# The seven products' sums on GpSimd, in another order, and a third seven-product chunk in five feed-forward layers

## The chip, the cores and the metric

The kernel runs on one core of a Trainium2 chip. The core has engines that run side by side, each with its own queue of instructions, worked off in order: TensorE (PE: matmuls; PEld: the load of the stationary operand), VectorE (DVE), ScalarE (ACT) and GpSimd (POOL), and SyncE (SP), which here issues the transfers from memory (DMA). They wait for each other by semaphores. SBUF is the on-chip memory, 128 partitions wide; PSUM is the small memory into which TensorE writes.

The metric is the device time of one execution in microseconds (us), as a median of runs.

## What is computed

One sequence of 256 tokens (two tiles t of 128 rows) with 1024 features goes through a first block and two layers of a second one, in float32:

```python
# first block
h = h + 0.5 * rms_norm(swiglu(rms_norm(h, g), w_gate, w_up, w_down), g2)   # f1
h = h + rms_norm(hybrid_mixer(rms_norm(h, g)), g2)    # attention and pooling, w_in 1024 x 4096
h = h + 0.5 * rms_norm(swiglu(...), g2)               # f2
h = h + rms_norm((p @ w_proj) * sigmoid(rms_norm(h, g) @ w_gate), g2)
# second block, i = 0, 1 (mixer: gated linear attention, then retention)
h = layer_norm(a * h + 0.5 * swiglu_2(h, ...))        # s0, s2
h = layer_norm(a * h + mixer(h))
h = layer_norm(a * h + 0.5 * swiglu_2(h, ...))        # s1, s3

def swiglu(x, w_gate, w_up, w_down):                  # 1024 -> 2816 -> 1024
    return (silu(x @ w_gate) * (x @ w_up)) @ w_down
```

So there are six feed-forward layers (f1, f2, s0 to s3). The other parts matter here only as neighbours.

## The kernel before

**Units and the three-matmul product.** The weights come in units of 128 x 2048 float32 (1 MB, four blocks of 128 rows by 512 columns). A unit is loaded into a `raw` buffer (five of them), ScalarE casts it to a rounded copy `whi` (float32r), VectorE subtracts that from `raw` and rounds the rest to `wlo` (`fetch`, lines 174 and 177; five buffers of each). The activations are split in the same way. `mm3` (lines 217 to 219) makes each product of three matmuls: hi by hi, hi by lo, lo by hi, 128x512 each.

**Chunks.** The gate and up products of a feed-forward layer have 5 chunks of 512 columns (0 to 4) and a last of 256 for each. A plain chunk takes four units (two halves of the 1024 rows, gate and up), and for both row tiles 4 x 2 x 4 x 3 = 96 matmuls.

**Seven products.** For the chunks in `SEVEN` (line 73; chunks 2 and 4 of f2 and s0 to s3) the two row tiles, the two halves of the inner dimension, and gate and up are taken as a 2 x 2 by 2 x 2 block product, made in the Strassen-Winograd way from seven products in place of eight (`seven`, lines 369 to 404): 7 x 4 x 3 = 84 matmuls. It needs sums of the four units a, b, c, d (`fetch_sum`, lines 182 to 198, table `SUMS`): in the order of the products a, a+b, b+c, a+b+c, c, d, a+b+c+d, where each of the four sums is a VectorE add in place (line 194), directly ahead of its cast (line 196) and subtraction (line 197). It also needs four differences of the activations (`sums_in`, lines 302 to 316), made and split on VectorE and ScalarE, once a layer. The products are combined on VectorE from PSUM (lines 392 to 402). Two pairs of column chunks of the mixer's input projection and two of the retention's go through the same functions (`Chunks.pair`, line 553), which makes 14 such groups in all.

**Order.** The program is written out in one order; each engine takes its own instructions in that order. `unit` (line 200) hands out the next unit and first issues the fetches up to four units ahead when a summed unit is near (line 204). `defer(n, f)` puts small work `n` ticks later (a tick is six matmuls), `settle` brings deferred work forward until a condition holds. In a seven-product chunk the finish (`finish7`, line 469) takes gate and up of one row tile together.

Of the kernel before, what the change touches and what calls it, by code (L numbers as in the profile page):

```python
# [11 lines left out]
F32 = mybir.dt.float32  # L12
# [3 lines left out]
AF = mybir.ActivationFunctionType  # L16
ALU = mybir.AluOpType
AX = mybir.AxisListType

P = 128  # L20
# [5 lines left out]
CW = 512  # L26
# [6 lines left out]
LAG = 3  # L33
POOL_WINDOWS = (2, 4, 8, 16)
EDGE = 8
SUMS = (("a", None), ("a", "b"), ("b", "c"), ("a", "c"), ("c", None), ("d", None), ("a", "d"))
AHEAD = 2
TURN = (5, 7)
SPIN = 9
# [12 lines left out]
def ffn_units(g, u, d, seven=()):  # L52


    out = []
    for c in range(5):
        four = [(g, 2 * c), (g, 2 * c + 1), (u, 2 * c), (u, 2 * c + 1)]
        out += [(four, j) for j in range(7)] if c in seven else four
    return out + [(g, 10), (g, 11)] + [(d, i) for i in range(11)]


def chunk_units(name, order):

    out = []
    for c in order:
        if isinstance(c, tuple):
            out += [([(name, 2 * b + i) for b in c for i in range(2)], j) for j in range(7)]
        else:
            out += [(name, 2 * c + i) for i in range(2)]
    return out  # L70


SEVEN = (2, 4)
MIX_ORDER = [1, 0, 2, 3, (4, 5), (6, 7)]
GLA_ORDER = [1, 0, 2, 4, 3, 5]
RET_ORDER = [2, 3, 0, 1, 4, 8, (5, 9), 6, 10, (7, 11)]
# [2 lines left out]
def all_units():  # L79

    p = ffn_units("f1g", "f1u", "f1d")
    p += chunk_units("bin", MIX_ORDER) + [("bpl", 0), ("bat", 0), ("bpl", 1), ("bat", 1)] + [("bout", i) for i in range(4)]
    p += ffn_units("f2g", "f2u", "f2d", SEVEN)
    p += [("pgate", i) for i in range(4)] + [("pproj", 0)]
    p += ffn_units("s0g", "s0u", "s0d", SEVEN)
    p += chunk_units("gin", GLA_ORDER) + [("gout", i) for i in range(4)]
    p += ffn_units("s1g", "s1u", "s1d", SEVEN) + ffn_units("s2g", "s2u", "s2d", SEVEN)
    p += chunk_units("rin", RET_ORDER) + [("rout", i) for i in range(8)]
    return p + ffn_units("s3g", "s3u", "s3d", SEVEN)


class Build:
# [89 lines left out]
    def fetch_sum(self, four, j):  # L182


        nc = self.nc
        if j == 0:
            self.sums = {}
        r = self.sums
        for key, at in {0: (("a", 0), ("b", 2)), 2: (("c", 3),), 5: (("d", 1),)}.get(j, ()):
            r[key] = self.T("raw", [P, UNIT], F32)  # L190
            nc.sync.dma_start(out=r[key], in_=self.ins[four[at][0]][four[at][1]])
        key, other = SUMS[j]
        if other:
            nc.vector.tensor_tensor(out=r[key], in0=r[key], in1=r[other], op=ALU.add)  # L194
        hi, lo = self.T("whi", [P, UNIT], F32R), self.T("wlo", [P, UNIT], F32R)
        nc.scalar.copy(hi, r[key])  # L196
        nc.vector.tensor_tensor(out=lo, in0=r[key], in1=hi.bitcast(F32), op=ALU.subtract)  # L197
        return Split(hi, lo)

    def unit(self, name, i, kb, ahead=1):  # L200
# [28 lines left out]
    def split(self, src, n=4, name="xT"):  # L229

        hi = self.S([P, n, P], F32R, name + "h")
        lo = self.S([P, n, P], F32R, name + "l")
        v = src[:, :n * P].rearrange("p (a b) -> p a b", a=n)
        self.nc.scalar.copy(hi, v)  # L234
        self.nc.vector.tensor_tensor(out=lo, in0=v, in1=hi.bitcast(F32), op=ALU.subtract)  # L235
        return Split(hi, lo)
# [62 lines left out]

        self.defer(TURN[t] + n + (more if raws is not None else 0), turn)  # L300

    def sums_in(self, raws, tag):

        a11, a12, a21, a22 = (raws.pop((t, n)) for t in range(NT) for n in range(2))
        y = {}
        for i, o, a, b in ((1, a22, a21, a22), (3, a21, a11, a21), (2, a11, a11, a22), (4, a12, a12, a11)):
            self.nc.vector.tensor_tensor(out=o, in0=a, in1=b, op=ALU.subtract)
            if i < 3:
                both = self.T(("gp", "gq")[i - 1], [P, 2, 4, P], F32R, name="yT")
                hi, lo = both[:, 0], both[:, 1]  # L310
            else:
                hi, lo = (self.T(tag, [P, CW], F32R, name=n).rearrange("p (a b) -> p a b", a=4) for n in ("yTh", "yTl"))
            self.nc.scalar.copy(hi, o)
            self.nc.vector.tensor_tensor(out=lo, in0=o, in1=hi.bitcast(F32), op=ALU.subtract)
            y[i] = Split(hi, lo)
        return y

    def rms_post(self, t, acc, gpost, half):

# [49 lines left out]
    def seven(self, x, y, four, done):  # L369

        nc, TT = self.nc, self.nc.vector.tensor_tensor
        t = lambda tag, name: self.T(tag, [P, CW], F32, name=name)

        def times(name, x, j):
            ps = self.M(name)
            w = self.unit(four, j, 4, 4)
            for k in range(4):
                self.mm3(ps, x[:, k, :], w[:, k, :], k == 0, k == 3)  # L380
                if k % 2:
                    self.tick()
            return ps

        p1, u2, u4, c22 = t("u", "p1"), t("u", "u2"), t("y", "u4"), t("y", "c22")
        nc.scalar.copy(p1, times("P1", x[0][0], 0))
        yield
        p5 = times("P5", y[1], 1)
        yield
        p7 = times("P7", y[3], 2)  # L390
        yield
        TT(out=u2, in0=times("P6", y[2], 3), in1=p1, op=ALU.subtract)
        TT(out=u4, in0=p5, in1=u2, op=ALU.add)
        TT(out=c22, in0=u4, in1=p7, op=ALU.subtract)
        TT(out=u2, in0=u2, in1=p7, op=ALU.subtract)
        yield
        TT(out=u4, in0=times("P3", y[4], 4), in1=u4, op=ALU.add)
        yield
        TT(out=p1, in0=times("P2", x[0][1], 5), in1=p1, op=ALU.add)
        done(0, p1, u4)  # L400
        yield
        TT(out=u2, in0=times("P4", x[1][1], 6), in1=u2, op=ALU.subtract)
        done(1, u2, c22)
        yield

    def lagged(self, x, name, n_units, after, lag=LAG, have=None, extra=None):
# [42 lines left out]
    def ffn(self, xT, r, wg, wu, wd, after, first=False, raws=None):  # L449
        nc = self.nc  # L450
# [16 lines left out]
                self.defer(4, lambda: hT.__setitem__((t, c), self.splitT(pr, n // P, "hT")))  # L467

        def finish7(c):
            prs = []  # L470

            def done(t, a, b):
                sg = self.T("sg", [P, CW], F32)
                pr = self.T("sg", [P, CW], F32, name="pr")
                nc.scalar.activation(sg, a, AF.Silu)
                nc.vector.tensor_tensor(out=pr, in0=b, in1=sg, op=ALU.mult)
                prs.append(pr)
                if t:
                    self.defer(4, lambda: turn(c, CW, *prs))

            return done

# [2 lines left out]
        def turn(c, n, *prs):  # L485
            tps = [self.transpose4(pr, n // P, "hT") for pr in prs]
            for t in range(NT):
                hT[t, c] = self.split(tps[t], n // P, "hT")

        pss, y = {}, {}  # L490
# [25 lines left out]
            finish(0, t, pss[t, wg], pss[t, wu], CW)  # L516
        for c in range(1, 6):
            if raws is not None and c == 1:
                self.defer(4, lambda: y.update(self.sums_in(raws, "ld")))
            if raws is not None and c in SEVEN:  # L520
                self.settle(lambda: y)
                for _ in self.seven(xT, y, [(wg, 2 * c), (wg, 2 * c + 1), (wu, 2 * c), (wu, 2 * c + 1)], finish7(c)):
                    pass
                continue
            for nm in (wg, wu) if c < 5 else (wg,):
                for i in range(2):
                    w = [self.unit(nm, 2 * c + i, 4, 3 if raws is not None else 2)]
                    for t in range(NT):
                        if i == 0:
                            pss[t, nm] = self.M()  # L530
                        self.proj(pss[t, nm], xT[t], w, CW, 4, 4 * i, KD)
                for t in range(NT):
                    if c == 5:
                        finish(c, t, pss[t, nm][:, :256], pss[t, nm][:, 256:], 256)
                    elif nm == wu:
                        finish(c, t, pss[t, wg], pss[t, wu], CW)
        self.lagged(lambda t, k: hT[t, k // 4][:, k % 4, :], wd, 11, after, have=lambda t, k: (t, k // 4) in hT)

    class Chunks:
# [8 lines left out]
            self.w, self.ps, self.over, self.y, self.groups = {}, {}, set(), {}, {}  # L548

        def sums(self):  # L550
            self.y.update(self.b.sums_in(self.raws, "S"))

        def pair(self, c):

            if c not in self.groups:
                self.b.settle(lambda: self.y)

                def done(t, *outs):
                    for i in range(2):
                        self.done(c[i], t, outs[i])  # L560
                        self.over.add((c[i], t))

                self.groups[c] = self.b.seven(self.xT, self.y, [(self.name, 2 * i + j) for i in c for j in range(2)], done)
            next(self.groups[c])
# [656 lines left out]
```

## Time and profile before

| | |
|---|---|
| median of three runs | 1611.38 us (1611.19 to 1611.48) |
| the profiled execution | 1611.8 us, span of its instructions 1610.0 us |
| granted TensorE clock, mean | 0.997 of full speed |
| busy share PE, DVE, ACT, POOL | 99, 77, 52, 7% |
| bytes read from memory | 305.86 MB, 191 GB/s over the span |

The span runs from the first to the last instruction. Matmuls are pipelined: one of 128x512 is shown with 0.39 us though the next begins earlier, so paces are read from starts, not from durations.

### The profile page before, as it was taken

The page shows a single profiled execution, that of the slowest core. Times are in us where ns is not written, and L with a number is a line of the kernel's source. Part 1 is how long each engine was busy: PE and PEld are TensorE (multiplying, and loading weights), DVE is VectorE, ACT ScalarE, POOL GpSimd, SP SyncE. Part 2 cuts the span into 40 slices and gives each one's busy share as a digit, 9 for nine tenths or more (in the row PEclk, how much of TensorE's full clock was granted, in tenths as well). Part 3 has the DMA queues.
Part 4 walks back from the last instruction along what each step waited for, and adds up shares of the span by engine and source line. Part 5 has one row for each costly group of instructions (what it writes and reads, how often), then busy time and mean ns, then how long its engine had stood idle before and what let it go on. Part 6 is the DMA issues. An engine that isn't in the chain of part 4 may idle for free. (4 is left out here: it accounts for less than half of the span.)

```text
span 1610.0 us, 18253 instructions
## 1 busy us (share of the span) xinstructions
PE 1589.4 (99%) x7353; PEld 1307.2 (81%) x7353; DVE 1233.6 (77%) x1086; ACT 836.7 (52%) x831; POOL 107.3 (7%) x102
## 2 busy tenths in 40 slices
PE   9999999999999999999999999999999999999997
PEld 6888877788888888888888888888887888788886
DVE  6654688978993789947648996699938899799954
ACT  7443555755663665634645563456634464456531
POOL 0000000000000100001022000100003401010000
PEclk9999999999999999999999999999999999999999
DMA  9764533654574455556534556544754543655550
GB/s 346 289 212 155 209 121 128 235 184 155 191 273 166 175 211 209 208 205 221 181 123 155 185 182 233 193 176 183 279 185 160 190 183 115 246 200 189 184 191 27
DMA packets 49797, 308.11 MB, mean 191 GB/s; under 512 B 6048, under 2 KB 7328, under 8 KB 15024
## 3 DMA queue, kind: packets, MB, share of 16 engines
q1 hardware_dynamic: 49568, 306.93, 52.6%
q8 instruction: 58, 0.95, 0.2%
q14 instruction: 27, 0.22, 0.0%
q10 hardware_dynamic: 144, 0.00, 0.0%
HBM read 305.86 MB, written 1.05 MB: 191 GB/s over the span
## 5 line engine op out<-in xcount | busy, mean ns | idle before, releaser
L177 DVE TENSOR_TENSOR wlo<-raw,whi 128x2048 fp32r<-128x2048 f32 (+1 forms) x231 | 503.1, 2185 | 247.1 <-ACT whi L174 247.0
L174 ACT CAST whi<-raw 128x2048 fp32r<-128x2048 f32 (+1 forms) x230 | 417.5, 1824 | 332.0 <-PE acc L219 190.5
L217 PE MATMUL mm<-whi,xTh 128*128 128x512 f32 x848 | 337.5, 398 | 0.2 <-ACT xTh L234 0.2
L219 PE MATMUL mm<-whi,xTl 128*128 128x512 f32 x848 | 331.4, 391 | 0.4 <-DVE xTl L235 0.4
L218 PE MATMUL mm<-wlo,xTh 128*128 128x512 f32 x848 | 331.3, 391 | 0.0
L196 ACT CAST whi<-raw 128x2048 fp32r<-128x2048 f32 x98 | 186.9, 1910 | 119.1 <-DVE raw L194 78.0
L197 DVE TENSOR_TENSOR wlo<-raw,whi 128x2048 fp32r<-128x2048 f32 x98 | 222.6, 2286 | 8.6 <-ACT whi L196 8.6
L217 PE MATMUL acc<-whi,hTh 128*128 128x512 f32 x528 | 207.0, 392 | 0.0
L219 PE MATMUL acc<-whi,hTl 128*128 128x512 f32 x528 | 205.6, 389 | 0.0
L218 PE MATMUL acc<-wlo,hTh 128*128 128x512 f32 x528 | 205.5, 389 | 0.0
L219 PEld LDWEIGHTS mm<-whi,xTl 128*128 128x128 f32 x848 | 159.2, 188 | 35.8 <-DVE xTl L235 1.8
L217 PEld LDWEIGHTS mm<-whi,xTh 128*128 128x128 f32 x848 | 159.3, 188 | 32.6 <-issue 0.8
L218 PEld LDWEIGHTS mm<-wlo,xTh 128*128 128x128 f32 x848 | 159.5, 188 | 31.1
L194 DVE TENSOR_TENSOR raw<-raw 128x2048 f32<-128x2048 f32 x56 | 128.3, 2291 | 0.1
L219 PEld LDWEIGHTS acc<-whi,hTl 128*128 128x128 f32 x528 | 99.1, 188 | 20.9
L218 PEld LDWEIGHTS acc<-wlo,hTh 128*128 128x128 f32 x528 | 99.2, 188 | 20.1
L217 PEld LDWEIGHTS acc<-whi,hTh 128*128 128x128 f32 x528 | 99.1, 188 | 20.1
L217 PE MATMUL mm<-whi,xh 128*128 128x512 f32 x176 | 69.0, 394 | 2.2 <-ACT whi L174 1.7
L218 PE MATMUL mm<-wlo,xh 128*128 128x512 f32 x176 | 68.8, 391 | 0.0
L219 PE MATMUL mm<-whi,xl 128*128 128x512 f32 x176 | 68.6, 390 | 0.0
L234 ACT CAST hTh<-hT 128x512 fp32r<-128x512 f32 (+1 forms) x72 | 38.6, 546 | 56.0 <-PE hT L226 55.8
L217 PE MATMUL P<-whi,xTh 128*128 128x512 f32 x168 | 66.3, 395 | 0.0
(261 smaller groups left out, 2105.5 us busy)
## 6 DMA issues: line engine op xcount, KB each, us to landing
raw<-in_rin SPq DMA_DIRECT2D x24, 1024.0 KB, 4.8
raw<-in_bin SPq DMA_DIRECT2D x16, 1024.0 KB, 4.8
raw<-in_f2g SPq DMA_DIRECT2D x12, 1024.0 KB, 4.8
raw<-in_s0g SPq DMA_DIRECT2D x12, 1024.0 KB, 4.8
raw<-in_gin SPq DMA_DIRECT2D x12, 1024.0 KB, 4.8
raw<-in_s1g SPq DMA_DIRECT2D x12, 1024.0 KB, 4.8
raw<-in_s2g SPq DMA_DIRECT2D x12, 1024.0 KB, 4.8
raw<-in_s3g SPq DMA_DIRECT2D x12, 1024.0 KB, 5.1
```

The source lines that it names most:

```text
L174: nc.scalar.copy(hi[:, s], raw[:, s])
L177: nc.vector.tensor_tensor(out=lo[:, s], in0=raw[:, s], in1=hi[:, s].bitcast(F32), op=ALU.subtract)
L194: nc.vector.tensor_tensor(out=r[key], in0=r[key], in1=r[other], op=ALU.add)
L196: nc.scalar.copy(hi, r[key])
L197: nc.vector.tensor_tensor(out=lo, in0=r[key], in1=hi.bitcast(F32), op=ALU.subtract)
L217: mm(ps, x.hi, w.hi, start=start, stop=False)
L218: mm(ps, x.hi, w.lo, start=False, stop=False)
L219: mm(ps, x.lo, w.hi, start=False, stop=stop)
L234: self.nc.scalar.copy(hi, v)
```

## The change

The sums of the units are made by GpSimd in place of VectorE, and they begin earlier: in the program, a+b is issued behind the fetch of the first unit, b+c behind the second, and (a+b)+c and d+(a+b+c) behind the third. The products' order becomes a, d, a+b, c, b+c, a+b+c, a+b+c+d (that is P1, P2, P5, P3, P7, P6, P4), and all four operands are loaded with the first two fetches. The four differences of the activations are made by GpSimd too, and their splits are deferred by 2 to 5 ticks. The finish of a seven-product chunk takes gate and up one at a time. `SEVEN` becomes (2, 3, 4), so chunk 3 of the five layers is made of seven products too.

```diff
-SUMS = (("a", None), ("a", "b"), ("b", "c"), ("a", "c"), ("c", None), ("d", None), ("a", "d"))
-SEVEN = (2, 4)
+SEVEN = (2, 3, 4)
@@ fetch_sum
-        for key, at in {0: (("a", 0), ("b", 2)), 2: (("c", 3),), 5: (("d", 1),)}.get(j, ()):
+        for key, at in {0: (("a", 0), ("b", 2)), 1: (("d", 1), ("c", 3))}.get(j, ()):
             r[key] = self.T("raw", [P, UNIT], F32)
             nc.sync.dma_start(out=r[key], in_=self.ins[four[at][0]][four[at][1]])
-        key, other = SUMS[j]
-        if other:
-            nc.vector.tensor_tensor(out=r[key], in0=r[key], in1=r[other], op=ALU.add)
+        src = r["adacbad"[j]]
         hi, lo = self.T("whi", [P, UNIT], F32R), self.T("wlo", [P, UNIT], F32R)
-        nc.scalar.copy(hi, r[key])
-        nc.vector.tensor_tensor(out=lo, in0=r[key], in1=hi.bitcast(F32), op=ALU.subtract)
+        nc.scalar.copy(hi, src)
+        nc.vector.tensor_tensor(out=lo, in0=src, in1=hi.bitcast(F32), op=ALU.subtract)
+        for o, i in {0: ("ab",), 1: ("bc",), 2: ("ac", "da")}.get(j, ()):
+            nc.gpsimd.tensor_tensor(out=r[o], in0=r[o], in1=r[i], op=ALU.add)
@@ sums_in
-        for i, o, a, b in ((1, a22, a21, a22), (3, a21, a11, a21), (2, a11, a11, a22), (4, a12, a12, a11)):
-            self.nc.vector.tensor_tensor(out=o, in0=a, in1=b, op=ALU.subtract)
+        def split(i, o):
...
             y[i] = Split(hi, lo)
-        return y
+        for n, (i, o, a, b) in enumerate(((1, a22, a21, a22), (3, a21, a11, a21), (2, a11, a11, a22), (4, a12, a12, a11))):
+            self.nc.gpsimd.tensor_tensor(out=o, in0=a, in1=b, op=ALU.subtract)
+            self.defer(2 + n, lambda i=i, o=o: split(i, o))
@@ seven
-        nc.scalar.copy(p1, times("P1", x[0][0], 0))
-        p5 = times("P5", y[1], 1)
-        p7 = times("P7", y[3], 2)
-        TT(out=u2, in0=times("P6", y[2], 3), in1=p1, op=ALU.subtract)
-        TT(out=u4, in0=p5, in1=u2, op=ALU.add)
-        TT(out=c22, in0=u4, in1=p7, op=ALU.subtract)
-        TT(out=u2, in0=u2, in1=p7, op=ALU.subtract)
-        TT(out=u4, in0=times("P3", y[4], 4), in1=u4, op=ALU.add)
-        TT(out=p1, in0=times("P2", x[0][1], 5), in1=p1, op=ALU.add)
-        done(0, p1, u4)
+        nc.scalar.copy(u2, times("P1", x[0][0], 0))
+        TT(out=c11, in0=times("P2", x[0][1], 1), in1=u2, op=ALU.add)
+        done(0, 0, c11)
+        self.settle(lambda: len(y) == 4)
+        p5 = times("P5", y[1], 2)
+        p3 = times("P3", y[4], 3)
+        p7 = times("P7", y[3], 4)
+        TT(out=u2, in0=times("P6", y[2], 5), in1=u2, op=ALU.subtract)
+        TT(out=c12, in0=p5, in1=u2, op=ALU.add)
+        TT(out=c22, in0=c12, in1=p7, op=ALU.subtract)
+        TT(out=u2, in0=u2, in1=p7, op=ALU.subtract)
+        TT(out=c12, in0=p3, in1=c12, op=ALU.add)
+        done(0, 1, c12)
+        done(1, 1, c22)
         TT(out=u2, in0=times("P4", x[1][1], 6), in1=u2, op=ALU.subtract)
-        done(1, u2, c22)
+        done(1, 0, u2)
```

## Rows read from the trace of the kernel before

**Rows 1.** The page: busy us (share of the span) and instructions by engine.
```profile
PE 1589.4 (99%) x7353; PEld 1307.2 (81%) x7353; DVE 1233.6 (77%) x1086; ACT 836.7 (52%) x831; POOL 107.3 (7%) x102
```
**Rows 2.** Waits of the weight loads: us in total, times, longest; products P.
```profile
PEld P L218 <- DVE wlo L197: 0.3, 1, 0.3
```
**Rows 3.** TensorE's timeline, s3 (start, us): first products of chunks 2, 3, 4, behind.
```profile
1466.22 0.39 PE L217 MATMUL P<-whi,xTh 128*128 128x512 f32 x1
...
1468.94 0.39 PE L217 MATMUL P<-whi,yT 128*128 128x512 f32 x1
...
1486.18 0.39 PE L217 MATMUL mm<-whi,xTh 128*128 128x512 f32 x1
...
1508.90 0.39 PE L217 MATMUL P<-whi,xTh 128*128 128x512 f32 x1
...
1528.84 0.39 PE L217 MATMUL mm<-whi,xTh 128*128 128x512 f32 x1
```
**Rows 4.** VectorE's groups by line: shapes, count | busy us, mean ns | idle before.
```profile
L197 DVE TENSOR_TENSOR wlo<-raw,whi 128x2048 fp32r<-128x2048 f32 x98 | 222.6, 2286 | 8.6 <-ACT whi L196 8.6
L194 DVE TENSOR_TENSOR raw<-raw 128x2048 f32<-128x2048 f32 x56 | 128.3, 2291 | 0.1
...
L402 DVE TENSOR_TENSOR u<-P,u 128x512 f32<-128x512 f32 x14 | 9.6, 685 | 0.0
```
**Rows 5.** VectorE's timeline, s3, chunks 1 and 2.
```profile
1446.53 2.28 DVE L197 TENSOR_TENSOR wlo<-raw,whi 128x2048 fp32r<-128x2048 f32 x1
...
1455.54 4.49 DVE L197 TENSOR_TENSOR wlo<-raw,whi 128x2048 fp32r<-128x2048 f32 x2
1459.95 2.28 DVE L194 TENSOR_TENSOR raw<-raw 128x2048 f32<-128x2048 f32 x1
...
1486.48 0.68 DVE L395 TENSOR_TENSOR u<-u,P 128x512 f32<-128x512 f32 x1
1487.08 0.69 DVE L397 TENSOR_TENSOR u<-P,u 128x512 f32<-128x512 f32 x1
```
**Rows 6.** GpSimd's timeline: adds and a product, with VectorE's two-tile passes away.
```profile
839.39 1.31 POOL L799 TENSOR_TENSOR gate<-gate,gnorm 128x512 f32<-128x512 f32 x1 [2.12 <-ACT gate L798]
...
1273.24 0.74 POOL L944 TENSOR_TENSOR rot<-ra,rb 128x256 f32<-128x256 f32 x1 [5.62 <-DVE rb L941]
1273.94 0.74 POOL L945 TENSOR_TENSOR rot<-rb,ra 128x256 f32<-128x256 f32 x1
```
**Rows 7.** Timelines of VectorE and GpSimd at one place of the retention.
```profile
1276.08 2.33 DVE L197 TENSOR_TENSOR wlo<-raw,whi 128x2048 fp32r<-128x2048 f32 x1 [0.69 <-ACT whi L196]
1278.45 2.71 DVE L194 TENSOR_TENSOR raw<-raw 128x2048 f32<-128x2048 f32 x1
...
1276.23 2.78 POOL L945 TENSOR_TENSOR rot<-rb,ra 128x256 f32<-128x256 f32 x1
```
**Rows 8.** The page: ScalarE's casts of summed units; columns as in rows 4.
```profile
L196 ACT CAST whi<-raw 128x2048 fp32r<-128x2048 f32 x98 | 186.9, 1910 | 119.1 <-DVE raw L194 78.0
```
**Rows 9.** TensorE's timeline: the mixer's first and past-last, the retention's two first products.
```profile
257.02 0.48 PE L217 MATMUL P<-whi,xTh 128*128 128x512 f32 x1
...
311.08 0.40 PE L217 MATMUL mm<-whi,plh 128*128 128x512 f32 x1
...
1304.06 0.39 PE L217 MATMUL P<-whi,xTh 128*128 128x512 f32 x1
...
1352.14 0.39 PE L217 MATMUL P<-whi,xTh 128*128 128x512 f32 x1
```
**Rows 10.** Stretches: us, busy us (count) of PE, PEld, DVE, ACT, POOL, PEclk, DMA share, GB/s.
```profile
5.00:10.00 5.00, 2.96 (x9) 1.55 (x10) 3.52 (x11) 3.69 (x11) 0.00 (x0) 1.00 0.83 261
```

More of the change, by code (lines that the diff above doesn't have):

```diff
@@ L300, in turn_in, with sums_in @@
         self.defer(TURN[t] + n + (more if raws is not None else 0), turn)
-    def sums_in(self, raws, tag):
+    def sums_in(self, raws, tag, y):
         a11, a12, a21, a22 = (raws.pop((t, n)) for t in range(NT) for n in range(2))
-        y = {}
-        for i, o, a, b in ((1, a22, a21, a22), (3, a21, a11, a21), (2, a11, a11, a22), (4, a12, a12, a11)):
-            self.nc.vector.tensor_tensor(out=o, in0=a, in1=b, op=ALU.subtract)
+        def split(i, o):
             if i < 3:
@@ L383, in times @@
             return ps
-        p1, u2, u4, c22 = t("u", "p1"), t("u", "u2"), t("y", "u4"), t("y", "c22")
-        nc.scalar.copy(p1, times("P1", x[0][0], 0))
+        u2, c11, c12, c22 = t("u", "u2"), t("u", "c11"), t("y", "c12"), t("y", "c22")
+        nc.scalar.copy(u2, times("P1", x[0][0], 0))
         yield
-        p5 = times("P5", y[1], 1)
+        TT(out=c11, in0=times("P2", x[0][1], 1), in1=u2, op=ALU.add)
+        done(0, 0, c11)
         yield
-        p7 = times("P7", y[3], 2)
+        self.settle(lambda: len(y) == 4)
+        p5 = times("P5", y[1], 2)
         yield
-        TT(out=u2, in0=times("P6", y[2], 3), in1=p1, op=ALU.subtract)
-        TT(out=u4, in0=p5, in1=u2, op=ALU.add)
-        TT(out=c22, in0=u4, in1=p7, op=ALU.subtract)
-        TT(out=u2, in0=u2, in1=p7, op=ALU.subtract)
-        yield
-        TT(out=u4, in0=times("P3", y[4], 4), in1=u4, op=ALU.add)
-        yield
-        TT(out=p1, in0=times("P2", x[0][1], 5), in1=p1, op=ALU.add)
-        done(0, p1, u4)
+        p3 = times("P3", y[4], 3)
+        yield
+        p7 = times("P7", y[3], 4)
+        yield
+        TT(out=u2, in0=times("P6", y[2], 5), in1=u2, op=ALU.subtract)
+        TT(out=c12, in0=p5, in1=u2, op=ALU.add)
+        TT(out=c22, in0=c12, in1=p7, op=ALU.subtract)
+        TT(out=u2, in0=u2, in1=p7, op=ALU.subtract)
+        TT(out=c12, in0=p3, in1=c12, op=ALU.add)
+        done(0, 1, c12)
+        done(1, 1, c22)
         yield
         TT(out=u2, in0=times("P4", x[1][1], 6), in1=u2, op=ALU.subtract)
-        done(1, u2, c22)
+        done(1, 0, u2)
         yield
@@ L469, in finish7, with done @@
         def finish7(c):
[L470 to L479, printed above, removed]
+            got, prs = {}, {}
+            def done(t, i, ps):
+                got[t, i] = ps
+                if i == 0:
+                    sg = got[t, 0] = self.T("sg", [P, CW], F32)
+                    nc.scalar.activation(sg, ps, AF.Silu)
+                if (t, 1 - i) in got:
+                    prs[t] = pr = self.T("sg", [P, CW], F32, name="pr")
+                    nc.vector.tensor_tensor(out=pr, in0=got[t, 1], in1=got[t, 0], op=ALU.mult)
+                if t and i == 0:
+                    self.defer(4, lambda: turn(c, CW, prs[0], prs[1]))
             return done
@@ L518, in ffn @@
             if raws is not None and c == 1:
-                self.defer(4, lambda: y.update(self.sums_in(raws, "ld")))
+                self.defer(4, lambda: self.sums_in(raws, "ld", y))
             if raws is not None and c in SEVEN:
-                self.settle(lambda: y)
                 for _ in self.seven(xT, y, [(wg, 2 * c), (wg, 2 * c + 1), (wu, 2 * c), (wu, 2 * c + 1)], finish7(c)):
@@ L550, in sums, with done @@
         def sums(self):
-            self.y.update(self.b.sums_in(self.raws, "S"))
+            self.b.sums_in(self.raws, "S", self.y)
         def pair(self, c):
             if c not in self.groups:
[L556 to L561, printed above, removed]
+                def done(t, i, ps):
+                    self.done(c[i], t, ps)
+                    self.over.add((c[i], t))
                 self.groups[c] = self.b.seven(self.xT, self.y, [(self.name, 2 * i + j) for i in c for j in range(2)], done)
```

## The prediction

> **What bounds the kernel now.** The page's busy table comes first: TensorE is busy for 1589.4 of 1610.0 us, VectorE for 1233.6, ScalarE for 836.7, GpSimd for 107.3 [rows 1]. A busy share can hide pauses, so the waits of TensorE and its weight loads are next: in the products of the seven-product chunks the longest wait on a converted weight is 0.3 us in total [rows 2]. TensorE is the bound everywhere, and the weights just keep up. The matmul timeline of the last feed-forward layer gives its pace: two successive products start 2.72 us apart (1466.22 to 1468.94), which is 0.2267 us for each of 12 matmuls; chunk 2 (seven products) takes 19.96 us, chunk 3 (plain) 22.72 us, chunk 4 (seven) 19.94 us, transposes included [rows 3].
>
> Behind TensorE stands the supply: each weight unit costs a cast on ScalarE (1.91 us [rows 8]) and a subtraction on VectorE (2.29 us); a summed unit also a VectorE add (2.29 us) [rows 4]. So a seven-product chunk asks VectorE for 7 + 4 such passes within 20 us. That has been hidden because a plain chunk follows and units are converted four ahead.
>
> **The change, part by part.**
>
> *Matmuls removed.* Chunk 3 of five layers goes from 96 matmuls to 7 x 4 x 3 = 84: 5 x 12 x 0.2267 = 13.6 us of TensorE time [rows 3]. That is on the path and is the whole possible gain.
>
> *VectorE relieved.* Its 56 adds of 2.29 us (128.3 us) go [rows 4]; by itself worth nothing, as TensorE did not wait for them.
>
> *GpSimd loaded.* 14 seven-product chunks become 19, with 4 sums each: 76 adds of 128x2048. The trace has none of that size. Two clean ones of 128x256 start 0.70 us apart and last 0.74 us, one of 128x512 lasts 1.31 us [rows 6]: 0.55 to 0.57 us for each further 256 elements. Estimate from these rows: 0.74 + 7 x 0.55 = 4.6 us, of which 8 x 0.55 = 4.4 us is streaming. Four are 18.4 us, under the 20 us of a chunk: GpSimd alone would keep up, and the sums begun two or three products (5.4 to 8.2 us) ahead would be in time.
>
> *The conflict.* What decides is whether GpSimd and VectorE run side by side. Both read their two operands from SBUF: the sum and the subtraction wlo<-raw,whi. Some 2 us after that clean pair GpSimd starts an add of 128x256 at 1276.23, while VectorE's subtraction runs from 1276.08 to 1278.41; the add, 0.74 us elsewhere, lasts 2.78 us and ends at 1279.01. VectorE's next pass, begun at 1278.45, takes 2.71 us in place of 2.29 [rows 6, 7]. GpSimd got nothing done beside the subtraction, and VectorE then stood for the 0.4 to 0.55 us of the add. They take turns, one whole instruction at a time.
>
> The rows show this for holds up to half a microsecond on GpSimd's side only. The Trainium skill (SBUF — State Buffer, section "Who interferes with whom") says that a VectorE instruction with two SBUF inputs contends with a GpSimd instruction that reads SBUF, and that the later one to issue blocks until the first has finished. By that rule a 4.4 us sum stops VectorE for 4.4 us, as in the sum below; without it only the first rival's 1598 us would be left. The trace agrees as far as it goes (2.78 us in place of 0.74).
>
> Price of the shared path per seven-product chunk: 4 sums x 4.4 = 17.6; 7 subtractions x 2.2 us start to start (4.41 us for two [rows 5]) = 15.4; together 33.0; the two gate products pr, of two SBUF tiles as before, 2 x 0.6 = 1.2 (pitch 0.6 [rows 5]). That is 34.2 us, against 20 us of TensorE. Before, the same work was on VectorE, 11 passes x 2.2 = 24.2, so moving the sums makes the joint load larger, not smaller.
>
> *Three in a row.* Now the layer. VectorE's subtraction for the first unit of chunk 2 starts at 1446.53 [rows 5]; this is the start of the window. TensorE would want the last unit of chunk 4 at 1466.22 + 3 x 19.95 - 2.72 = 1523.35 [rows 3]. Room: 76.8 us. Needed on the shared path: 3 x 33.0 + 2 x 1.2 for the pr of chunks 2 and 3 + about 3 for what of the activation sums (four GpSimd subtractions of 128x512, about 1.1 us each by [rows 6], and their splits) falls into the window = 104.4 us. TensorE waits at least 27.6 us per layer. Most of it falls in chunks 3 and 4; in chunk 2 the 20 us of lookahead nearly cover.
>
> To this come gaps in which the path stands idle: the cast of a summed unit (1.91 us) starts only after its sum, and VectorE's 9 passes per chunk with a PSUM operand (7 combinations of products and 2 splits of transposes, 0.6 each, 5.4 us [rows 4, 5]) stand in order between the subtractions. They run free beside a GpSimd sum, but a subtraction that waits blocks those behind it. Between none and all (3 x 5.4 = 16.2 us) I take some 2 us per chunk, nearer the lower end, since sums fill over half of the path's time: 6.4, so 34 us per layer, 170 in all.
>
> After chunk 4 nothing more is late: plain units need 2.2 us of VectorE each for 5.4 us of TensorE.
>
> *Mixer and retention.* Their four seven-product groups also get GpSimd sums. The mixer's two take from 257.02 to 311.08, 54 us, other work included, after a long lead; the retention's start at 1304.06 and 1352.14 with 48 us between [rows 9]. 2 x 34.2 = 68 us against 54 plus at least 20 of lead, and 34.2 against 48: no standing shortage. What can be late is work queued behind: VectorE's softmax and normalisation passes stand behind a blocked subtraction, and GpSimd's small powers behind a 4.4 us sum; VectorE in turn waits for those. Between 0 and 30 us; I take 10, some two or three blocked turns per group.
>
> *The rest.* The sums' reordering, the earlier loads of the fourth and third operand, the split of the gate's finish into halves and the deferral of the activations' splits move instructions without adding any. I cost them at 0: DMA and ScalarE (16 us per 20 us chunk at most: 7 x 1.91 and a few of 0.6 [rows 8]) have room. If they did not, it would add to the gaps above.
>
> **Sum**, against the profiled execution (1611.8 us, span 1610.0): 1611.8 - 13.6 + 170 + 10 = 1778.2; the median of the runs is 0.4 lower, so **1778 us**.
>
> **Rivals.**
>
> *1. The long sums do not hold VectorE up* (the other side). If GpSimd gives way inside an instruction, VectorE needs 21 x 2.2 + 3 x (5.4 + 1.2) = 66 us of the 76.8, all hidden, and only the removed matmuls count: 1611.8 - 13.6 = **1598 us**. For it: no row shows a long sum. Against: GpSimd's add of 128x256 made no headway during a subtraction, and VectorE's pass grew by most of the add's time [rows 7]. It decides if a sum costs VectorE under about 2 us. Chance 0.12.
>
> *2. A sum blocks for half its length*, 2.2 us: the path needs 3 x 24.2 + 5.4 = 78 us against 76.8, so only the gaps remain, 1.2 + 6.4 = 7.6 us per layer: 1611.8 - 13.6 + 38 = **1636 us**. For it: VectorE's 2.71 is 0.42 above 2.29, a little less than the whole add. Chance 0.05.
>
> *3. The pauses also cost TensorE its clock.* If the granted clock falls to 1.2 GHz while TensorE is only half busy, a product takes 5.4 us and a chunk 38.1, more than the path's 35: about 10 us more per layer, **1828 us**. Against: between 5 and 10 us TensorE was busy for 2.96 of 5 us at a granted clock of 1.00 [rows 10]. Chance 0.06.
>
> **How the numbers follow.** The forecast has 0.77. Its own range: low, without gaps and with half of the 27.6 us made up by lead that I don't count (13.6 x 5 = 68, nothing in the mixers), 1611.8 - 13.6 + 68 = 1666; high, if none of the PSUM passes is covered (43.8 x 5 = 219) and the mixers cost 30, 1847, and 1865 with a part of rival 3's price on top. So 1665 to 1865 holds 0.8; the rest lies below, but for some of rival 3. Faster by over 0.2% (3.2 us, about what can be told from no change here): rival 1, 0.12. Same: 0.02, from rival 2's lower edge. Slower: 0.86.
>
> **What would show it.** In the trace after: GpSimd's 76 adds, median near 4.6 us where VectorE is quiet and 6 to 7 us where it has to wait a turn; VectorE's subtractions in chunks 2 to 4 with a mean well over 2.29 us, many at 6 to 7 us; TensorE waiting for wlo and whi in P3, P2 and the later products, some 30 us per layer in chunks 3 and 4, little in chunk 2; the five layers each longer by about 31 us, the GLA stretch, which has no such group, unchanged. The prediction is wrong if the subtractions stay at 2.3 us beside running sums, or if TensorE stays without waits; and its size is wrong if the adds take much less or more than 4.6 us.

## The result, and the profile after

The changed kernel takes 1846.22 us (median of 4 runs, 1845.34 to 1847.18) against 1611.29 us before: a ratio of 1.1458, 95% interval 1.1438 to 1.1478. That is slower, as forecast, by 235 us in place of 167, and inside the range, at its upper end.

The page after, first the busy time by engine and the costliest groups that are new (columns as in [rows 1, 4]):

```profile
PE 1646.8 (89%) x7293; PEld 1335.6 (72%) x7293; DVE 1360.9 (74%) x1052; ACT 862.9 (47%) x851; POOL 573.1 (31%) x206
...
L196 POOL TENSOR_TENSOR raw<-raw 128x2048 f32<-128x2048 f32 x76 | 419.3, 5517 | 273.0 <-DVE wlo L194 270.0
L194 DVE TENSOR_TENSOR wlo<-raw,whi 128x2048 fp32r<-128x2048 f32 x133 | 443.2, 3351 | 66.3 <-ACT whi L193 66.0
```

The 60 matmuls are gone (7353 to 7293), and TensorE is busy for 89% in place of 99% [rows 1]. Its idle time grew by 178 us (20.6 to 198.1), its busy time by 57 us although there are fewer matmuls: its mean granted clock was 0.944 in place of 0.997, and a matmul at the lower clock is shown with 0.63 us in place of 0.39. VectorE lost 56 adds (128.3 us) and is still busy for 127 us more. Its subtraction of a summed unit, of which chunk 3 adds 35, went from 2286 ns [rows 4] to a mean of 3351 ns, which is 142 us for all 133.

Where the time went, by stage: each stage has a small power on GpSimd in its last normalisation, and the distance between the starts of these (those of the first row tile), against the kernel before, is (us; "layers" is the mean of f2, s0, s1, s2, s3, whose differences lie within 3 us of each other in every kernel shown; the kernels that were not yet named are those of the experiments below):

| kernel | layers, each | mixer | retention | f1, ple, GLA |
|---|---|---|---|---|
| changed | +41.7 | +7.1 | +20.4 | 0 |
| sums on VectorE | +22.2 | +3.8 | +7.8 | +1 |
| two chunks | +14.6 | +7.1 | +19.8 | 0 |
| write-only | +6.0 | +3.1 | +9.7 | 0 |
| quarters | +49.0 | +2.2 | +21.3 | 0 |
| order only | 0.0 | +3.9 | +6.8 | 0 |
| before, three chunks | +21.5 | 0.0 | -0.7 | 0 |

TensorE's timeline of the changed kernel in s3, the first products of chunks 2, 3 and 4 and the first matmul of chunk 5 [rows 3], with what it waited for:

```profile
1660.08 0.39 PE L216 MATMUL P<-whi,xTh 128*128 128x512 f32 x1
...
1684.36 0.73 PE L216 MATMUL P<-whi,xTh 128*128 128x512 f32 x1 [2.29 <-DVE u L399]
...
1722.43 0.39 PE L216 MATMUL P<-whi,xTh 128*128 128x512 f32 x1
...
1762.91 0.77 PE L216 MATMUL mm<-whi,xTh 128*128 128x512 f32 x1 [4.12 <-DVE u L399]
```

Chunk 2 takes 24.3 us (19.96 before), chunk 3 38.1 (22.72, plain), chunk 4 40.5 (19.94). The waits are mostly not on weights, as I had thought they would show, but one step further on (the longest of TensorE's waits in the whole run; us, times, longest):

```profile
PE hT L225 <- DVE pr L484: 54.1, 11, 6.3
PE P L216 <- DVE c L400: 39.4, 5, 8.2
PE P L216 <- DVE u L402: 26.9, 5, 5.5
PE mm L216 <- DVE u L399: 20.5, 5, 4.1
PE P L216 <- DVE u L399: 11.5, 5, 2.3
PE gT L225 <- DVE on L971: 7.2, 3, 4.9
```

L399, L400 and L402 are VectorE's combinations of products. A product that waits for them wants their PSUM bank (there are five). In VectorE's queue they stand behind subtractions. At 1689.98 such a subtraction has first waited 5.76 us for its cast, which waited for its sum, and then lasts 4.79 us because it also waits its turn beside the next sum; c<-P,u (L400) comes only after it. pr, which the transposes hT need, stands there too, and as it reads two SBUF tiles it also waits its own turn (1739.05).

The turns themselves, in VectorE's timeline of s3 and then GpSimd's (x2: two sums in a row; GpSimd's waits for wlo are not turns: a sum is made in place and has to wait until the subtraction has read its tile):

```profile
1642.44 2.28 DVE L194 TENSOR_TENSOR wlo<-raw,whi 128x2048 fp32r<-128x2048 f32 x1
1644.64 0.68 DVE L312 TENSOR_TENSOR yT<-xr,yT 128x512 fp32r<-128x512 f32 x1
1645.25 5.10 DVE L312 TENSOR_TENSOR yTl<-xr,yTh 128x512 fp32r<-128x512 f32 x1
1650.27 6.70 DVE L194 TENSOR_TENSOR wlo<-raw,whi 128x2048 fp32r<-128x2048 f32 x1
...
1689.98 4.79 DVE L194 TENSOR_TENSOR wlo<-raw,whi 128x2048 fp32r<-128x2048 f32 x1 [5.76 <-ACT whi L193]
1694.69 0.68 DVE L400 TENSOR_TENSOR c<-P,u 128x512 f32<-128x512 f32 x1
...
1732.88 0.68 DVE L403 TENSOR_TENSOR c<-P,c 128x512 f32<-128x512 f32 x1
1733.48 5.65 DVE L194 TENSOR_TENSOR wlo<-raw,whi 128x2048 fp32r<-128x2048 f32 x1
1739.05 4.98 DVE L484 TENSOR_TENSOR pr<-c,sg 128x512 f32<-128x512 f32 x1
...
1753.27 2.28 DVE L194 TENSOR_TENSOR wlo<-raw,whi 128x2048 fp32r<-128x2048 f32 x1
```
```profile
1644.80 10.02 POOL L196 TENSOR_TENSOR raw<-raw 128x2048 f32<-128x2048 f32 x2 [7.84 <-DVE wlo L194]
1659.85 13.21 POOL L196 TENSOR_TENSOR raw<-raw 128x2048 f32<-128x2048 f32 x2 [5.03 <-DVE wlo L194]
1681.49 11.13 POOL L196 TENSOR_TENSOR raw<-raw 128x2048 f32<-128x2048 f32 x2 [8.44 <-DVE wlo L194]
1694.85 11.08 POOL L196 TENSOR_TENSOR raw<-raw 128x2048 f32<-128x2048 f32 x2 [2.23 <-DVE wlo L194]
1719.02 11.18 POOL L196 TENSOR_TENSOR raw<-raw 128x2048 f32<-128x2048 f32 x2 [13.09 <-DVE wlo L194]
1732.44 11.04 POOL L196 TENSOR_TENSOR raw<-raw 128x2048 f32<-128x2048 f32 x2 [2.23 <-DVE wlo L194]
```

yT and yTl are the same operation on the same size. One ran ahead of the sum, the other was issued 0.45 us after it: 0.68 against 5.10 us, 4.42 us longer. The next subtraction takes 6.70 = 2.28 + 4.42: one whole further sum. In contrast c<-P,c (L403), with one operand in PSUM, takes its 0.68 us while a sum runs. The pairs of a+b and b+c start 36.7 and 37.5 us apart: that is the pace of a chunk.

### The profile page after: what moved, and what is told of

The parts are those of the page before. It is cut to its first block, busy times and chain, and to the rows that moved or that the text cites. A ratio compares the mean times of both kernels' runs of the same rounds, so it can differ in the third digit from the quotient of the medians.

```text
span 1844.9 us, 18404 instructions
## 1 busy us (share of the span) xinstructions
PE 1646.8 (89%) x7293; PEld 1335.6 (72%) x7293; DVE 1360.9 (74%) x1052; ACT 862.9 (47%) x851; POOL 573.1 (31%) x206
## 5 line engine op out<-in xcount | busy, mean ns | idle before, releaser
L176 DVE TENSOR_TENSOR wlo<-raw,whi 128x2048 fp32r<-128x2048 f32 (+1 forms) x211 | 458.5, 2186 | 284.3 <-ACT whi L173 284.1
L173 ACT CAST whi<-raw 128x2048 fp32r<-128x2048 f32 (+1 forms) x210 | 379.4, 1815 | 375.3 <-PE acc L218 199.8
L196 POOL TENSOR_TENSOR raw<-raw 128x2048 f32<-128x2048 f32 x76 | 419.3, 5517 | 273.0 <-DVE wlo L194 270.0
L194 DVE TENSOR_TENSOR wlo<-raw,whi 128x2048 fp32r<-128x2048 f32 x133 | 443.2, 3351 | 66.3 <-ACT whi L193 66.0
L193 ACT CAST whi<-raw 128x2048 fp32r<-128x2048 f32 x133 | 251.7, 1903 | 321.3 <-POOL raw L196 231.2
L216 PE MATMUL mm<-whi,xTh 128*128 128x512 f32 x688 | 280.0, 407 | 20.8 <-DVE u L399 20.5
L218 PE MATMUL mm<-whi,xTl 128*128 128x512 f32 x688 | 274.0, 399 | 0.4 <-DVE xTl L234 0.4
L217 PE MATMUL mm<-wlo,xTh 128*128 128x512 f32 x688 | 272.6, 396 | 0.0
L216 PE MATMUL P<-whi,xTh 128*128 128x512 f32 x228 | 95.7, 420 | 50.8 <-DVE c L400 39.4
L217 PE MATMUL P<-wlo,xTh 128*128 128x512 f32 x228 | 94.3, 414 | 3.6 <-DVE wlo L194 3.6
L218 PE MATMUL P<-whi,xTl 128*128 128x512 f32 x228 | 93.6, 410 | 0.0
```

Source lines behind the costliest of these rows:

```text
L173: nc.scalar.copy(hi[:, s], raw[:, s])
L176: nc.vector.tensor_tensor(out=lo[:, s], in0=raw[:, s], in1=hi[:, s].bitcast(F32), op=ALU.subtract)
L193: nc.scalar.copy(hi, src)
L194: nc.vector.tensor_tensor(out=lo, in0=src, in1=hi.bitcast(F32), op=ALU.subtract)
L196: nc.gpsimd.tensor_tensor(out=r[o], in0=r[o], in1=r[i], op=ALU.add)
L216: mm(ps, x.hi, w.hi, start=start, stop=False)
```

## The experiments

Theory: GpSimd's sums and VectorE's passes over two SBUF tiles take turns, each for a whole instruction. Rival A: three seven-product chunks in a row are too much, whoever sums. Rival B: a GpSimd sum is merely long, and what waits for it comes late. Rival C: a single long turn holds up what stands behind it.

**Sums on VectorE, all else as changed.**

```diff
-            nc.gpsimd.tensor_tensor(out=r[o], in0=r[o], in1=r[i], op=ALU.add)
+            nc.vector.tensor_tensor(out=r[o], in0=r[o], in1=r[i], op=ALU.add)
...
-            self.nc.gpsimd.tensor_tensor(out=o, in0=a, in1=b, op=ALU.subtract)
+            self.nc.vector.tensor_tensor(out=o, in0=a, in1=b, op=ALU.subtract)
```

> The changed kernel with its 76 sums and the activations' differences back on VectorE; order, early loads and three chunks kept. Theory (GpSimd and VectorE take turns on the second SBUF read path, each for a whole instruction): the turns are gone, what is left is VectorE alone with 11 passes of 2.2 us, 1.2 of pr and 5.4 of PSUM passes per chunk, 94 us of work in a window of 76.8 us, 17 us of waiting less 2.7 us of removed matmuls per layer, nothing in mixer and retention: about 1684 us (1640 to 1710). Rival A (three chunks in a row are too much for the supply, whoever makes the sums): about as long as the changed kernel, 1846 us. Rival B (only the length of a GpSimd sum delays the casts): also much shorter, and not told from the theory here.

Measured: 1729.08 us, ratio to before 1.0738 (1.0719 to 1.0756). VectorE's groups by line:

```profile
L194 DVE TENSOR_TENSOR wlo<-raw,whi 128x2048 fp32r<-128x2048 f32 x133 | 302.6, 2285 | 14.3 <-ACT whi L193 13.7
L196 DVE TENSOR_TENSOR raw<-raw 128x2048 f32<-128x2048 f32 x76 | 174.1, 2290 | 0.4
```

The subtraction is back at 2285 ns: the turns are gone, and 117 us with them. But 1729 is above both my 1684 and its range: Rival A has the other half. VectorE now makes 174 us of adds that GpSimd made in the changed kernel, and the kernel is still 117 us shorter.

**Two chunks, sums on GpSimd.**

```diff
-SEVEN = (2, 3, 4)
+SEVEN = (2, 4)
```

> The changed kernel with chunk 3 plain again: the sums stay on GpSimd, for 14 groups. Theory (turns): the path needs 2 x 33 + 4 x 2.2 + 2 x 1.2 + 3 = 80 us in a window of 79.6, so only gaps and a late first chunk remain, 5 to 10 us per layer, and the 27 us lost in mixer and retention stay: 1663 to 1690 us, slower than before although no chunk was added. Rival A (three in a row is the trouble): at or under 1640 us. VectorE's subtractions of summed units still have a mean near 3.3 us by the theory.

Measured: 1710.51 us, 1.0618 (1.06 to 1.0635), above the expected range and far above Rival A's. The subtraction has a mean of 3458 ns here (x98). So with the number of chunks as before, the sums on GpSimd (with their order) cost 99 us; the gaps were again larger than allowed for, 14.6 us per layer in place of 5 to 10.

**GpSimd occupied, but reading nothing.** (The sums are left out.)

```diff
-            nc.gpsimd.tensor_tensor(out=r[o], in0=r[o], in1=r[i], op=ALU.add)
+            for _ in range(2):
+                nc.gpsimd.memset(r[o], 0.0)
```

> Each sum on GpSimd replaced by two memsets of the same 128x2048 tile, so the sums are left out: GpSimd is still occupied for some 4 us at the same place and the same casts wait for it, but it reads nothing from SBUF. Theory (turns on the read path): VectorE's subtractions fall back to 2.29 us, VectorE needs 66 us of the 76.8 us window, TensorE doesn't wait: 1598 to 1615 us. Rival B (what costs is that a GpSimd sum is long and the casts and products wait for it): nearly unchanged, over 1780 us. If writes take turns as well, between 1700 and 1846 us.

Measured: 1650.12 us, 1.0245 (1.023 to 1.026). One line each of VectorE's groups, of GpSimd's memsets (ns min/median/max) and of TensorE's waits:

```profile
L194 DVE TENSOR_TENSOR wlo<-raw,whi 128x2048 fp32r<-128x2048 f32 x133 | 302.9, 2287 | 54.1 <-ACT whi L193 53.4
...
L197 POOL MEMSET raw<- x152: 1801/1814/1840, 208.0 to 1551.1; 128x2048 f32 x152
...
PE mm L217 <- DVE u L400: 22.5, 5, 4.5
```

GpSimd is busy for 2 x 1.8 = 3.6 us at each sum's place, and VectorE's subtraction doesn't notice: mean 2287, longest 2383 ns. Rival B's over 1780 us did not come; these writes take no turns. A cast waits for the memsets as for a sum, and VectorE waits 53 us for such casts (66 in the changed kernel), as Rival B has it; but the whole run loses only 39 us. So of the 235 us, 196 hang on what a sum does beyond this (reading, and its further 0.9 us, which this run does not tell apart). What is left, 39 us, is above my 1598 to 1615: the order costs 10 us (below), and at the end of chunk 4 TensorE waits 4.5 us a layer for a bank. Argued, not shown: VectorE's 22 us per chunk against TensorE's 20 add up over three chunks; the total fits the window, but a combination late by a few us holds a bank.

**Sums in quarters.**

```diff
-            nc.gpsimd.tensor_tensor(out=r[o], in0=r[o], in1=r[i], op=ALU.add)
+            for q in range(4):
+                s = slice(q * CW, (q + 1) * CW)
+                nc.gpsimd.tensor_tensor(out=r[o][:, s], in0=r[o][:, s], in1=r[i][:, s], op=ALU.add)
```

> Each GpSimd sum cut into four of 128x512, same work, so that a turn lasts 1.1 us in place of 4.4 us. Theory (the total time of the turns bounds): the path still needs 33 us and some dispatch per chunk; 1800 to 1850 us, and no VectorE subtraction over 3.5 us. Rival C (what costs beyond the total is that VectorE's PSUM passes are stuck behind one long turn): shorter by most of the 10 us per layer and 17 us in the mixers that the forecast missed, 1780 to 1800 us.

Measured: 1882.15 us, 1.1678 (1.1661 to 1.1695), 36 us longer than the changed kernel. Both expected times missed; that no subtraction lasts over 3.5 us held. VectorE's subtraction (ns min/median/max), a group of VectorE, GpSimd's timeline in s3, and TensorE's longest waits:

```profile
L194 DVE TENSOR_TENSOR wlo<-raw,whi x133: 2274/2293/3423, 224.6 to 1785.0; 128x2048 fp32r<-128x2048 f32 x133
...
L486 DVE TENSOR_TENSOR pr<-c,sg 128x512 f32<-128x512 f32 x30 | 25.9, 865 | 97.6 <-ACT sg L483 97.6
...
1749.01 28.35 POOL L198 TENSOR_TENSOR raw<-raw 128x512 f32<-128x512 f32 x16 [11.72 <-DVE wlo L194]
...
PE hT L227 <- DVE pr L486: 97.1, 16, 10.1
PE P L218 <- DVE c L402: 30.4, 5, 6.5
PE P L219 <- DVE wlo L194: 17.5, 5, 3.5
PE mm L218 <- DVE u L401: 14.4, 5, 3.4
PE P L218 <- DVE u L404: 13.0, 5, 3.2
...
PE P L218 <- DVE u L401: 3.3, 4, 1.1
```

The longest subtraction is 3.42 = 2.28 + 1.14 us, one quarter more: the turn is the instruction, whatever its length. What Rival C names is there: TensorE's waits for banks that VectorE's combinations hold fall from 98 us (39.4 + 26.9 + 20.5 + 11.5 in the changed kernel) to 61. But a chunk's four sums now take 28.4 us from first to last in place of 24.5 (1719.02 to 1743.48), since VectorE can come in between quarters (a quarter lasts from 1.25 us up to 3.40). The casts wait longer, and ScalarE works in order: the gate's silu (sg) behind a waiting cast is late (VectorE waits 97.6 us for it), so pr, the transposes (97.1 us in place of 54.1) and TensorE. Shorter turns traded VectorE's holding time for a later sum, and the loss was larger than the gain. Nor does the total time of the turns, which is nearly the same here, set the kernel's time by itself.

**The order alone.** Both edits: sums on VectorE, two chunks.

> The changed kernel's order of products, early loads and split finish alone: sums and differences on VectorE, chunks 2 and 4. If the new order is free, as the forecast had it: only mixer and retention longer, by the 3.8 and 7.8 us that they show with the sums on VectorE, 1611 to 1628 us. If the order itself costs the layers something (write-only sums left 9 us of waiting per layer): 1640 to 1665 us.

Measured: 1621.98 us, 1.0066 (1.0049 to 1.0083). The five layers are unchanged to 0.1 us; mixer and retention take 3.9 and 6.8 us more. In the layers the new order, the early loads and the halved finish are free; in the two mixers they are not.

**Three chunks alone**, in the kernel before.

```diff
-SEVEN = (2, 4)
+SEVEN = (2, 3, 4)
```

> The kernel before with chunk 3 made of seven products too, nothing else: old order, sums on VectorE. Theory (VectorE then has 94 us in a window of 76.8): 17 less 2.7 us per layer, 1684 us (1660 to 1700). If three in a row alone cost what the run with the new order and VectorE sums showed (22 us per layer): 1720 us; then the new order is free in the layers.

Measured: 1720.31 us, 1.0674 (1.0658 to 1.069): 21.5 us per layer, where the new order had 22.2. TensorE's two longest waits in sum, and one of VectorE's:

```profile
PE P L217 <- ACT whi L196: 31.4, 26, 2.5
PE P L218 <- DVE wlo L197: 27.1, 20, 1.9
...
DVE wlo L197 <- ACT whi L196: 24.0, 27, 1.3
```

Here it does wait for weights, in many small pieces. VectorE has no long pause, but from chunk 2 of s3 on it stands seven times for 0.6 to 1.4 us, 6.9 us together: 3.7 for a cast that waited for the sum ahead of it, the rest for a product or for a transpose's cast. That is about the 7 us per layer that the sum of the passes left out.

**The clock**, first a control with one transpose bank less, then idle matmuls into that bank (`spin(18)` issues 18 of them; its code is left out below).

```diff
-    BUFS = {"raw": 5, "whi": 5, "wlo": 5, "S": 28, "mm": 5, "tp": 3, "y": 2, "u": 2,
+    BUFS = {"raw": 5, "whi": 5, "wlo": 5, "S": 28, "mm": 5, "tp": 2, "sp": 1, "y": 2, "u": 2,
```

> Control for the next run: the changed kernel with two PSUM banks for transposes in place of three, the third left unused. Expected within 10 us of the changed kernel's 1846 us if the transposes' banks are not what TensorE waits for; over 1860 us if they are.

```diff
+            if four[0][1] in (6, 8) and four[0][0] not in ("bin", "rin"):
+                self.spin(18)
             ps = self.M(name)
```

> The control with 18 idle matmuls of 128x256 bf16 (about 2 us) into the unused bank ahead of each product of chunks 3 and 4 of the five layers, 14 us per chunk of some 38, so that TensorE pauses less and its granted clock should stay up; they change no result. If the lower clock in these chunks (0.73 and 0.79 of full) is on the path: shorter than the control by 15 to 40 us. If the shared path of VectorE and GpSimd sets the pace and the clock costs nothing: the same within 5 us, or longer by what the idle matmuls delay.

Measured: control 1848.00 us, 1.1465 (1.1447 to 1.1482), as the changed kernel; with idle matmuls 1898.57, 1.1777 (1.176 to 1.1795). Chunks 3 and 4 in s3, of the control and with idle matmuls, columns as in [rows 10] (the granted clock is the third number from the right):

```profile
1686.04:1724.05 38.01, 27.11 (x92) 21.43 (x93) 31.25 (x19) 15.71 (x12) 22.53 (x5) 0.73 0.31 111
1724.05:1764.54 40.49, 25.19 (x94) 19.55 (x92) 34.28 (x20) 21.33 (x15) 18.73 (x4) 0.79 0.43 145
```
```profile
1727.41:1776.58 49.17, 38.04 (x193) 29.95 (x193) 41.67 (x21) 21.09 (x15) 32.06 (x7) 0.79 0.25 86
1776.58:1816.81 40.23, 35.21 (x203) 28.04 (x201) 31.02 (x22) 14.22 (x12) 9.34 (x2) 0.92 0.57 203
```

In the first half of chunk 3 the idle matmuls run at once and the pause comes after them (TensorE waits 6.7 us for a bank, 6.6 in the control). In its second half TensorE has no pause to fill, and they stand in line: the chunk takes 49.2 us in place of 38.0, which over five layers is about the 50 us. In chunk 4 the clock rose from 0.79 to 0.92, and the chunk takes 40.2 us in place of 40.5, idle matmuls included. GpSimd's last two pairs of sums took from 1761.39 to 1786.00, 24.6 us, and 24.5 in the control (1720.70 to 1745.16): the pace of the sums did not follow the clock. So the clock's own price is not settled; shown is that a higher clock in chunk 4 did not speed the sums up.

No run points to a version that beats the kernel before: every one with a third chunk or with sums on GpSimd is slower, and the order alone gains nothing.

## Why the prediction was right, and where its sizes were off

**The account.** From the medians, step by step: order 1611.8 to 1622.0 (+10), third chunk with sums on VectorE 1622.0 to 1729.1 (+107), sums to GpSimd 1729.1 to 1846.2 (+117). The runs that take one part alone: the third chunk in the old order +109; GpSimd on two chunks +89 over the order alone. So the third chunk costs 107 to 109 us with the sums on VectorE and 136 (1710.5 to 1846.2) with them on GpSimd: some 28 us belong to both parts together.

**The step that decided**, that a sum stops VectorE for its whole length, is shown three ways: the same pass at 0.68 and 5.10 us, the longest subtraction at 2.28 plus one sum and, with quarters, plus one quarter, and no effect from a GpSimd that only writes. The rule of the Trainium skill (SBUF — State Buffer, section "Who interferes with whom") holds here for turns of 4.42 us, where [rows 7] could show half a microsecond. Rival 1 (no hold) and rival 2 (half of it) fall. Rival 1 also had its own time wrong: with the hold gone and no sums on VectorE the kernel took 1650, not 1598 us.

**The length of a sum**, 4.6 us from adds of 256 and 512 columns: the shortest of 76 took 4.51 us; with turns the mean is 5.52.

**Removed matmuls**, 13.6 us: 60 fewer, as said; too little to be seen apart in any run.

**Waiting per layer**, 34 us: measured 41.7 + 2.7 = 44.4. The joint path was right: from the first subtraction of chunk 2 to the end of chunk 4's last I had 104.4 + 6.4 = 110.8 us, and in s3 it takes 113.1 (1642.44 to 1755.55), at a pace of 36.7 and 37.5 us per chunk. So of VectorE's 5.4 us of PSUM passes per chunk about 3 are not covered, where I took 2. Two things were not in the sum. That first subtraction leads TensorE by 17.6 us in place of 19.7, and at the end of chunk 4 TensorE waits 4.1 us more for a bank whose combination stands behind subtractions of later units; I had said that after chunk 4 nothing is late. The three make 8.5 of the 10.4 us that were missing per layer; the rest is not assigned. Chunk 2, said to be nearly covered, loses 4.3 us of it all. That the result lies by the upper bound of that term, 43.8, is luck: the bound took all 5.4 us as not covered and had none of the other two.

**Mixer and retention**, 10 us: measured 27.5 (7.1 + 20.4), and 10.7 us of it is the order, a step that I had put at 0. The rest, 16.8, fits the reason given without being divided by any run: in the retention VectorE now waits for small powers on GpSimd (5.6 us for rr), and TensorE for what follows (7.2 us, gT behind L971). The two terms, 5 x 10.4 and 17.5 us, are about the 68 us that the forecast was short by.

**What the profile was to show**: the subtractions and GpSimd's waits came much as described (in s3 seven of 21 subtractions last 4.8 to 6.7 us, the others 2.3). TensorE's waits did not: I named wlo and whi, and it waits for banks and transposes, one step behind the same cause. Rival 3's event came (the clock fell to 0.73 in chunk 3), in spite of [rows 10]. Its price stays open: with the removed 13.6 us, TensorE's busy time grew by 71 us, of which I had nothing in the sum. But in chunks 3 and 4 of s3 each stretch at the lower clock is followed by a further wait for VectorE, and VectorE for its part waits for transposes only 1.1 and 1.8 us. That chunk 3 takes 38.1 us, as rival 3 had it, is luck: it had the clock at half and no waits.

**What the account adds**: the forecast blamed the shared path for all of it. By the runs, almost half is the third chunk, which with the sums on VectorE already asks that engine for 31 us and some pauses per 20 us of TensorE. Moving the sums did not relieve it; it doubled the loss.

## What to carry to other kernels

Ahead of moving a pass from VectorE to GpSimd, look whether the passes that stay read two SBUF tiles: if so, each of them that meets the GpSimd instruction can wait for its whole length (4.4 us here, for a moved pass of 2.2), and relief on paper is extra load. Cost a queue by its order, not by its total: what fits a window in sum can still hold a PSUM bank or a cast a few us too long. And cutting the long instruction up does not help while the one who waits for the whole sum is the next bottleneck.

## What the runs showed of the hardware that was not expected

GpSimd's memset of 128x2048 (1.81 us) beside VectorE's two-tile passes cost these nothing (2287 ns), while a sum that also reads held them for 4.42 us. In the control's chunk 3 the granted clock was 0.73 with TensorE shown busy for 27.1 of 38 us, while at the start [rows 10] 2.96 of 5 us had left it at 1.00. Within chunk 3 of the changed kernel it was 0.50, the lower of its two levels (1.2 and 2.4 GHz), from 1695 to 1701 us, behind a pause of 6.6 us, with matmuls 0.43 us apart; from 1712 to 1727 us, without a pause, it was 1.00, with matmuls 0.23 us apart.
